# Interleaving two arrays: the store queue opens with loads in place of a tiny write

## The chip, the cores and the metric

The kernel runs on one core of one Trainium2 chip. The metric is device time in microseconds (us); where several executions were timed, the median is quoted with the lowest and highest.

## The reference

```python
def reference(x, y):                      # both (32, 256, 1024) float32
    result = np.zeros((batch, seq, dim * 2), dtype=np.float32)
    result[..., 0::2] = x
    result[..., 1::2] = y
    return result
```

The kernel reads 67.11 MB and writes 67.11 MB. There is no arithmetic.

## The kernel before

The arrays are flattened and cut into 8 tiles of 128 partitions by 8192 columns, 4.19 MB each. SyncE issues the loads of x and y, VectorE copies x into the even and y into the odd columns of an output tile (half an input tile at a time, so an output tile has 4.19 MB too), and ScalarE's sequencer (ACT) issues the stores. There are two buffers each for x, y and output.

```python
    xpool = ctx.enter_context(tc.tile_pool(name="xp", bufs=2))
    ypool = ctx.enter_context(tc.tile_pool(name="yp", bufs=2))
    opool = ctx.enter_context(tc.tile_pool(name="op", bufs=2))
    ...
    zero = wpool.tile([16, 128], fp32, name="zero")      # the early tiny write, 8 KB
    nc.vector.memset(zero, 0.0)
    first = dataclasses.replace(of, offset=0, ap=[[2 * WL, 16], [1, 128]])
    nc.scalar.dma_start(out=first, in_=zero)

    for lw in lwidths:
        ...
        nc.sync.dma_start(out=xtile, in_=xs)
        nc.sync.dma_start(out=ytile, in_=ys)
        while soff < lw:
            ...
            nc.vector.tensor_copy(out=otile[:, 0::2], in_=xsub)
            nc.vector.tensor_copy(out=otile[:, 1::2], in_=ysub)
            nc.scalar.dma_start(out=os_, in_=otile)
```

After compilation, the first load (x of the first tile) is moved ahead of the start barrier, into the opening block of SyncE.

## Time and profile before

| | before |
|---|---|
| time, median of 3 runs (lowest to highest) | 316.19 us (315.69 to 316.49) |
| span of the profiled execution | 313.8 us |
| the two queues' packets, share of 16 DMA engines | 99.4% |
| VectorE busy | 23% |
| first store issued, landed | 24.3 us, 48.1 us |

The table says that the 16 DMA engines are the bound and hardly ever idle. The page's lines and the stretches of the span that show it stand in the prediction below, with their reading. One more view belongs here, the timeline of the opening. Its columns are start, duration, engine, line, operation, output and input, count, and in brackets the wait before it.

```profile
12.28 4.50 DVE L70 COPY otile<-xtile 128x4096 f32<-128x4096 f32 x2 [11.25 <-DMA xtile<-in_x_dram]
...
22.00 4.50 DVE L71 COPY otile<-ytile 128x4096 f32<-128x4096 f32 x2 [5.22 <-DMA ytile<-in_y_dram]
24.32 33.66 ACTq L72 DMA_DIRECT2D out_dram<-otile  x3
```

VectorE copies x as soon as it is there, 10 us before y, and the first store is issued at 24.32, after the first copy of y.

### The profile page before, as it was taken

How to read it: one execution, taken by the hardware profiler on the slowest of the kernel's cores; microseconds unless marked ns; L12 is line 12 of the kernel's file. 1: busy time of each engine (PE TensorE's matmuls, PEld its weight loads, DVE VectorE, ACT ScalarE, POOL GpSimd, SP SyncE). 2: the span in 40 equal slices, each digit the busy share in tenths (PEclk: the TensorE clock that was granted, in tenths of full speed). 3: DMA queues.
4: the chain of work that ended last, by engine and by line, in shares of the span. 5: the costliest groups of instructions: out<-in, count | busy, mean ns of one | idle time of the engine just before them, and what ended most of it. 6: DMA issues, size and time to landing. Idle time of an engine off the chain costs nothing.

```text
span 313.8 us, 152 instructions
## 1 busy us (share of the span) xinstructions
DVE 72.8 (23%) x33; POOL 0.2 (0%) x4
## 2 busy tenths in 40 slices
DVE  0433002231032410325003150130501305023500
POOL 0000000000000000000000000000000000000000
DMA  8999999999999999999999999999999999999997
GB/s 339 464 405 397 468 401 464 405 464 405 464 405 464 405 459 409 451 418 451 418 434 434 430 439 426 443 413 455 401 468 401 468 401 468 401 468 401 464 405 334
DMA packets 4640, 134.23 MB, mean 428 GB/s; under 512 B 528, under 2 KB 544, under 8 KB 544
## 3 DMA queue, kind: packets, MB, share of 16 engines
q1 hardware_dynamic: 2304, 67.11, 49.9%
q10 hardware_dynamic: 2336, 67.12, 49.5%
HBM read 67.11 MB, written 67.12 MB: 428 GB/s over the span
## 4 chain that ended last, share of the span: by engine, by line
DMA 83%; DVE 11%; DVEq 1%; issue 0%
DMA out_dram<-otile 76%; DMA ytile<-in_y_dram 7%; DVE otile L71 6%; DVE otile L70 5%; DVEq L83 1%; DVEq L70 0%
## 5 line engine op out<-in xcount | busy, mean ns | idle before, releaser
L70 DVE COPY otile<-xtile 128x4096 f32<-128x4096 f32 x16 | 36.6, 2295 | 184.9 <-DMA out_dram<-otile 173.7
L71 DVE COPY otile<-ytile 128x4096 f32<-128x4096 f32 x16 | 36.6, 2292 | 39.8 <-DMA ytile<-in_y_dram 39.8
L45 DVE MEMSET zero<- 16x128 f32 x1 | 0.2, 165 | 0.9 <-PEq L119 0.9
L119 POOL MEMSET const-bfloat16-1.0<- 128x1 bf16 x1 | 0.1, 102 | 0.0
L119 POOL MEMSET const-uint8-127<- 128x1 uint8 x1 | 0.1, 102 | 0.0
L119 POOL MEMSET const-float32-0.0<- 128x1 f32 x1 | 0.1, 99 | 0.2 <-issue 0.2
L119 POOL MEMSET const-float32-1.0<- 128x1 f32 x1 | 0.1, 99 | 0.0
## 6 DMA issues: line engine op xcount, KB each, us to landing
out_dram<-otile ACTq DMA_DIRECT2D x16, 4096.0 KB, 29.1
xtile<-in_x_dram SPq DMA_DIRECT2D x8, 4096.0 KB, 43.6
ytile<-in_y_dram SPq DMA_DIRECT2D x8, 4096.0 KB, 60.7
out_dram<-zero ACTq DMA_DIRECT2D x1, 8.0 KB, 6.3
```

The costliest lines, as they stand in the source:

```text
L45: nc.vector.memset(zero, 0.0)
L70: nc.vector.tensor_copy(out=otile[:, 0::2], in_=xsub)
L71: nc.vector.tensor_copy(out=otile[:, 1::2], in_=ysub)
L83: tc.compile()
L119: nc = _bacc.Bacc("TRN2", target_bir_lowering=False, num_devices=1)
```

## The change

The intent: the ACT queue does useful work from the opening on, so the tiny write that opened it early is dropped. Both queues load from the start: x of the first tile on SyncE and y of the first tile on ACT, both ahead of the start barrier; then x and the second half of y of the second tile on SyncE, the first half of that y on ACT.

```diff
-    zero = wpool.tile([16, 128], fp32, name="zero")
-    nc.vector.memset(zero, 0.0)
-    first = dataclasses.replace(of, offset=0, ap=[[2 * WL, 16], [1, 128]])
-    nc.scalar.dma_start(out=first, in_=zero)
 ...
-        nc.sync.dma_start(out=xtile, in_=xs)
-        nc.sync.dma_start(out=ytile, in_=ys)
+        if t != 1:
+            nc.sync.dma_start(out=xtile, in_=rows(xf, start, lw))
+            yq = nc.scalar if t == 0 else nc.sync
+            yq.dma_start(out=ytile, in_=rows(yf, start, lw))
+        if t == 0:
+            nxt = start + P * lw
+            ...
+            nc.sync.dma_start(out=nx, in_=rows(xf, nxt, lw))
+            nc.scalar.dma_start(out=ny[:, :H], in_=rows(yf, nxt, lw, H))
+            nc.sync.dma_start(out=ny[:, H:], in_=rows(yf, nxt + H, lw, H))
 ...                                   # after compilation
-        if i.engine == mybir.EngineType.SP and i.opcode == "DMACopy"
+    for engine in (mybir.EngineType.SP, mybir.EngineType.Activation):
+        ...                           # the first DMA of each goes into its opening block
```

More of the change, by code (lines that the diff above doesn't have):

```diff
@@ L40, in _interleave, with rows @@
     assert sum(lwidths) == total // P
-    wpool = ctx.enter_context(tc.tile_pool(name="wp", bufs=1))
-    zero = wpool.tile([16, 128], fp32, name="zero")
-    nc.vector.memset(zero, 0.0)
-    first = dataclasses.replace(of, offset=0, ap=[[2 * WL, 16], [1, 128]])
-    nc.scalar.dma_start(out=first, in_=zero)
-    start = 0
-    for lw in lwidths:
-        xtile = xpool.tile([P, WL], fp32, name="xtile")[:, :lw]
-        ytile = ypool.tile([P, WL], fp32, name="ytile")[:, :lw]
-        xs = dataclasses.replace(xf, offset=start, ap=[[lw, P], [1, lw]])
-        ys = dataclasses.replace(yf, offset=start, ap=[[lw, P], [1, lw]])
-        nc.sync.dma_start(out=xtile, in_=xs)
-        nc.sync.dma_start(out=ytile, in_=ys)
-        soff = 0
-        while soff < lw:
-            width = min(WS, lw - soff)
-            otile = opool.tile([P, 2 * WS], fp32, name="otile")[:, : 2 * width]
+    H = WL // 2
+    def rows(flat, at, pitch, width=None):
+        return dataclasses.replace(flat, offset=at, ap=[[pitch, P], [1, width or pitch]])
+    start = 0
+    held = None
+    for t, lw in enumerate(lwidths):
+        if held is None:
+            xtile = xpool.tile([P, WL], fp32, name="xtile")
+            ytile = ypool.tile([P, WL], fp32, name="ytile")
+        else:
+            xtile, ytile = held
+            held = None
+        if t != 1:
[4 more added lines that the diff above has]
+            nxt = start + P * lw
+            nx = xpool.tile([P, WL], fp32, name="xtile")
+            ny = ypool.tile([P, WL], fp32, name="ytile")
+            nc.sync.dma_start(out=nx, in_=rows(xf, nxt, lw))
+            nc.scalar.dma_start(out=ny[:, :H], in_=rows(yf, nxt, lw, H))
+            nc.sync.dma_start(out=ny[:, H:], in_=rows(yf, nxt + H, lw, H))
+            held = nx, ny
+        for soff in range(0, lw, WS):
+            otile = opool.tile([P, 2 * WS], fp32, name="otile")
             os_ = dataclasses.replace(
@@ L65, in _interleave @@
                 offset=2 * start + 2 * soff,
-                ap=[[2 * lw, P], [1, 2 * width]],
+                ap=[[2 * lw, P], [1, 2 * WS]],
             )
-            xsub = xtile[:, soff : soff + width]
-            ysub = ytile[:, soff : soff + width]
-            nc.vector.tensor_copy(out=otile[:, 0::2], in_=xsub)
-            nc.vector.tensor_copy(out=otile[:, 1::2], in_=ysub)
+            nc.vector.tensor_copy(
+                out=otile[:, 0::2], in_=xtile[:, soff : soff + WS]
+            )
+            nc.vector.tensor_copy(
+                out=otile[:, 1::2], in_=ytile[:, soff : soff + WS]
+            )
             nc.scalar.dma_start(out=os_, in_=otile)
-            soff += width
         start += P * lw
@@ L86 @@
     blocks = nc.main_func.blocks
-    opening = blocks[0].instructions
-    at, moved = next(
-        (b, i)
-        for b in blocks[1:]
-        for i in b.instructions
-        if i.engine == mybir.EngineType.SP and i.opcode == "DMACopy"
-    )
-    assert not moved.sync_info.on_wait
-    body = at.instructions
-    body.remove(moved)
-    gate = next(
-        n
-        for n, i in enumerate(opening)
-        if i.engine == mybir.EngineType.SP and i.opcode == "Drain"
-    )
-    opening.insert(gate, moved)
-    at.instructions = body
-    blocks[0].instructions = opening
+    for engine in (mybir.EngineType.SP, mybir.EngineType.Activation):
+        opening = blocks[0].instructions
+        at, moved = next(
+            (b, i)
+            for b in blocks[1:]
+            for i in b.instructions
+            if i.engine == engine and i.opcode == "DMACopy"
+        )
+        assert not moved.sync_info.on_wait
+        body = at.instructions
+        body.remove(moved)
+        gate = next(
+            n
+            for n, i in enumerate(opening)
+            if i.engine == engine and i.opcode == "Drain"
+        )
+        opening.insert(gate, moved)
+        at.instructions = body
+        blocks[0].instructions = opening
 _INS = ['x', 'y']
```

## The prediction

> **What bounds the kernel now.** I read the page first: the row of DMA tenths, then the DMA queues, then the chain that ended last; after that the trace cut into stretches that begin and end on rows of transfers.
>
> The page, its slices and its queues:
>
> ```profile
> DVE  0433002231032410325003150130501305023500
> ...
> DMA  8999999999999999999999999999999999999997
> ...
> q1 hardware_dynamic: 2304, 67.11, 49.9%
> q10 hardware_dynamic: 2336, 67.12, 49.5%
> HBM read 67.11 MB, written 67.12 MB: 428 GB/s over the span
> ```
>
> The reader is to see that the DMA engines are 90% busy or more in every slice but the first and the last, while VectorE, the only computing engine, is at 23%. The two queues' packets took 49.9 + 49.5 = 99.4% of 16 engines' 313.8 us, that is 311.9 us. The kernel moves each byte once in and once out, and the change moves the same ones (but for 8 KB).
>
> The chain that ended last, on the page:
>
> ```profile
> DMA 83%; DVE 11%; DVEq 1%; issue 0%
> DMA out_dram<-otile 76%; DMA ytile<-in_y_dram 7%; DVE otile L71 6%; DVE otile L70 5%; DVEq L83 1%; DVEq L70 0%
> ```
>
> The chain names VectorE for 11%, but this is a trap: it follows one buffer from hand to hand, and while VectorE copies, the DMA engines carry other transfers (the slices show it). What ends the kernel is the time the 16 engines need for 134.23 MB, plus the moments in which they move nothing or are slow.
>
> Those moments come from the stretches. Columns: the stretch, its length, VectorE, GpSimd, clock, DMA share (1.00 is all 16 engines busy), GB/s.
>
> ```profile
> 0.00:0.90 0.90, 0.04 (x1) 0.20 (x4) 1.00 0.00 0
> 0.90:4.05 3.15, 0.13 (x1) 0.00 (x0) 1.00 0.99 333
> 4.05:25.80 21.75, 8.30 (x4) 0.00 (x0) 1.00 1.01 434
> 25.80:29.05 3.25, 0.69 (x1) 0.00 (x0) 1.00 0.94 323
> 29.05:312.60 283.55, 63.61 (x28) 0.00 (x0) 1.00 1.00 433
> 312.60:313.80 1.20, 0.00 (x0) 0.00 (x0) 1.00 0.00 0
> ```
>
> Loads alone run at 434 GB/s, loads beside stores and stores alone at 433: one ceiling whatever the mix. At 433 GB/s the data takes 134.23 / 0.433 = 310.0 us. The rest is four losses: 0.9 us before the first packet; 3.15 x (1 - 333/433) = 0.73 us in the first row of packets; 3.25 x (1 - 323/433) = 0.83 us where the first large store enters; 1.2 us after the last packet. Sum 313.7, the span to 0.1. So everything that any re-ordering can win is 3.7 us, or 1.2%, and this change touches about half of that.
>
> **What the Trainium skill says.** "DMA: Bandwidth & Descriptors", section "Where 436 GB/s comes from", puts the ceiling of the 16 ports at 435.2 GB/s; the trace agrees with 433 to 434. The same page, "Issuing engines are not separate DMA queues", says that transfers issued from several engines run on the same 16 DMA engines and interleave, and that issuing from several only saves the sequencer's time. The trace agrees: one queue alone (4.05 to 25.80) and two together (29.05 on) have the same rate. The same page, "Queues, rings and completion order", says that an engine takes turns between its queues, a packet at a time; the before fits that (the first store, issued at 24.32, landed by 48.1, some 24 us, where alone it would have had 4.19 MB / 0.433 = 9.7). I use it below to place transfers.
>
> **The change, part by part.** The order of instructions on each engine shows what moves. Removed: a VectorE memset (0.17 us, beside the DMA) and the tiny 8 KB write. Moved: y0 from SyncE to the opening of the ACT queue; the first half of y1 onto the ACT queue, the second half last on SyncE. VectorE's first four copies go from x, x, y, y to x, y, x, y. From the second tile on all stays.
>
> (1) *Bytes.* 8 KB less of 134.23 MB: 0.02 us at 433 GB/s. y1 in halves makes 128 more packets (8 per engine) of 16 KB instead of 32. With 4640 packets in all and the four losses explaining all but 0.1 us, a packet's fixed cost must be small: if all of that 0.1 were fixed cost, 290 packets per engine would have 0.3 ns each. I set +0.05 us as a generous estimate. Net 0.
>
> (2) *First data.* Before, x0 alone lands at 12.3 and y0 at 22.0. After, x0 and y0 take turns and both land near 22 (same 8.39 MB, 19.4 us, after the same start). VectorE starts its first copy about 10 us later, and the first store can be issued after two copies of 2.29 us, less their overlap 4.5 us: at 26.5 instead of 24.3. No DMA time is lost by it, because both queues still hold loads: x1 and both halves of y1, 8.39 MB or 19.4 us, until about 41.
>
> (3) *First store.* It stands behind the first half of y1 in the ACT queue. From 22, x1 (4.19 MB) and that half (2.10 MB) take turns: 6.29/0.433 = 14.5 us, both done near 36.5. Then the second half and store 0: 14.5 us, to 51. Then x2 and store 1, y2 and store 2, and so on, 19.4 us each. So the first store enters at 36 instead of 29, and the kernel is behind in stores by 7 us or so, and ahead in loads by as many bytes.
>
> (4) *The tail.* Following the pairs, x2 with store 1 ends at 51 + 19.4 = 70.4, and eleven more pairs bring y7 in at 70.4 + 11 x 19.4 = 284 (before: 287.7). Three stores remain, 3 x 9.7 = 29.1, to 313. The store of the first half of tile 7 is issued 4.5 us after 284, while store 13 runs until 293.5; the last is issued 4.5 us after 293.5, while store 14 runs until 303. Slack 5 us at each: the queue doesn't run dry, the tail costs nothing.
>
> (5) *The entry of the store queue*, the only place where I expect a gain. The 0.83 us at 25.80 to 29.05 comes once, when the ACT queue gets its first large transfer; later stores have no such dip. After, that queue is at work from the opening on. If the loss belongs to the queue's waking, it goes or coincides with SyncE's own 0.73 at the start: -0.8. If it belongs to the first write to HBM, it stays. I can't tell from the before, and take half: -0.4.
>
> (6) *The start.* ACT issues y0 in about 0.4 us beside SyncE's x0, which has 0.37; the start barrier may go back by 0.1, which only later issues feel. The 0.9 us before the first packet and the 1.2 us at the end stay.
>
> Sum: 0.0 + 0.0 + 0.0 + 0.0 - 0.4 + 0.0 = -0.4 us on 316.19: **315.8 us**.
>
> **The rivals.** *A: the whole dip goes.* For it: it occurs once and at the queue's first large transfer. Against: the tiny write had already woken the queue at about 5 us and the dip came all the same. Time: 315.4. *B: the tiny write did pay.* It may have spared the first store a longer stall, which now comes back at 36 us: for it, that someone put it in; against, that a y load has the queue moving by then. The dip would double, +0.8: 317.0. *C: two loads in turn are slower than one load stream*, through HBM or through both queues opening cold: the stretch of loads alone lasts from 1 to 36 us; 1% less rate there is +0.35, a second cold row +0.7: 316.5 to 316.9. For it, nothing but that no such stretch is in the before; against, that every mix there runs at 433. *D: VectorE, waiting until 22 us for its first input, becomes a bound.* It is busy for 72.8 us of 313.8 and its copies need 9.2 us of each 38.7 us tile; the shift of 10 us would have to reach the store queue while that is empty, and by (3) it isn't. Nothing.
>
> **Range and chances.** A gives the low side (315.4, and by the spread of the runs before, 315.69 to 316.49, about 0.4 lower: 315.0), B and C the high side (316.9). Faster by over 2% means under 309.9 us, below the 310.0 that the data alone needs: 1%, left for an effect on the DMA rate itself. Slower by over 2% is over 322.5: it needs 6 us of idle DMA, which the placing of transfers excludes unless I have a dependence wrong: 2%. Within 2%: 97%.
>
> **What would show it.** In the stretches of the changed kernel: no packet before 0.9; a first row at about 330 GB/s; 433 to 434 from there to the first store; at about 36 us a dip to 320 GB/s over 3 us (it stayed) or none (A); 433 to the last 1.2 us. The waits: VectorE waits some 21 us once for x or y at the start. The first store issued near 26.5, landing near 51; the last store issued 14 us before the end. The queues' share summed should be 99.4 to 99.8%. Wrong would be a stretch of over 1 us with the DMA idle in the middle or the tail, a rate between 1 and 36 us other than 433, or two slow first rows.

## The result

| | before | after |
|---|---|---|
| time, median of 6 runs (lowest to highest) | 316.03 us (315.69 to 316.49) | 316.12 us (316.01 to 316.28) |
| span of the profiled execution | 313.8 us | 314.4 us |
| first store issued, landed | 24.3, 48.1 us | 26.4, 52.4 us |
| y of the last tile is there | 287.7 us | by 284.9 us |

The ratio is 1.0002, with a 95% interval of 0.9989 to 1.0015: the same time. (A ratio here is the mean time of one kernel's fast runs over that of the other's in the same rounds, so it isn't quite the ratio of the medians quoted.) The after is no faster, but it is steadier: its six runs lie within 0.27 us, those of before within 0.80 us. The profile of before had fallen on one of its fastest executions (315.62 us), which makes the spans look further apart than the medians are.

The last row of the table rests on these two lines, the first copy that needs y of the last tile before, and the first copy of the last tile after. The latter waited for an output buffer, so its input was there earlier:

```profile
287.67 2.29 DVE L71 COPY otile<-ytile 128x4096 f32<-128x4096 f32 x1 [4.92 <-DMA ytile<-in_y_dram]
284.86 2.29 DVE L79 COPY otile<-xtile 128x4096 f32<-128x4096 f32 x1 [14.95 <-DMA out_dram<-otile]
```

The page of the changed kernel, slices, packets and queues:

```profile
DVE  0029003205041050410505004050140502305500
...
DMA  9999999999999999999999999999999999999997
...
DMA packets 4752, 134.22 MB, mean 427 GB/s; under 512 B 528, under 2 KB 528, under 8 KB 528
...
q10 hardware_dynamic: 2592, 73.40, 54.2%
q1 hardware_dynamic: 2160, 60.82, 45.2%
```

The DMA row is 9 everywhere but in the last slice, VectorE starts in the third slice instead of the second, and the ACT queue (q10) now carries 54.2% against 45.2% on SyncE's (q1). The sum, 99.4%, is that of before.

The same cut into stretches as the prediction has for the kernel before (stretch, length, VectorE, GpSimd, clock, DMA share, GB/s):

```profile
0.00:0.90 0.90, 0.00 (x0) 0.20 (x4) 1.00 0.00 0
0.90:3.93 3.03, 0.00 (x0) 0.00 (x0) 1.00 0.99 346
3.93:33.60 29.67, 8.90 (x4) 0.00 (x0) 1.00 1.00 433
33.60:37.10 3.50, 0.00 (x0) 0.00 (x0) 1.00 1.05 300
37.10:313.25 276.15, 62.96 (x28) 0.00 (x0) 1.00 1.00 432
313.25:314.40 1.15, 0.00 (x0) 0.00 (x0) 1.00 0.00 0
```

Loads alone on two queues run at 433 GB/s for 30 us. The dip at the first store has moved from 26 to 34 us and is still there: 3.50 x (1 - 300/433) = 1.08 us, against 0.83 before. The slow first row of packets has shrunk a little: 3.03 x (1 - 346/433) = 0.61 us, against 0.73.

And the opening of the changed kernel in its timeline:

```profile
0.12 0.38 ACTq L62 DMA_DIRECT2D ytile<-in_y_dram  x1
...
21.84 2.30 DVE L79 COPY otile<-xtile 128x4096 f32<-128x4096 f32 x1 [21.84 <-DMA xtile<-in_x_dram]
...
26.37 50.32 ACTq L85 DMA_DIRECT2D out_dram<-otile  x4
```

VectorE waits 21.84 us once, since x and y of the first tile now arrive together, and the first store is issued 2 us later than before.

**A finer reading of the same traces.** A stretch cuts through rows of packets, because the 16 engines do not run in step. The trace has every packet with its start and duration, and an engine's next packet starts where its last one ended (up to 4 ns before), so the packets can be strung into 16 chains. A packet of 32 KB takes 1.213 us in all traces when nothing disturbs it (one of 16 KB takes 0.611), and in the kernel before each engine has exactly 256 of them: 310.5 us. What an engine takes above that is its own loss. For the dip I sum that loss from 20 to 45 us. The end of each chain is marked by that engine's completion of the last store. Which chain a packet belongs to is not certain where two engines end within a few ns of each other, so a loss is not given engine by engine; the mean and the ends do not depend on it. In its place stands the time of the slowest packet in the dip above its usual 1.213 or 0.611. In us (the mean dip is some 0.06 low, since packets overlap by a few ns):

```
kernel            first store   dip per engine   slowest packet,   end of the 16 engines    span
                  enters        mean             above usual       median   last
before (fast run)   29.1        0.58             0.67              312.41   312.70          313.8
after               37.1        1.14             0.78              312.92   313.24          314.4
```

In the kernel before 21 packets are stretched in the dip, in the changed kernel 46, by about as much each. In both they are loads, and all of them start before the first packet of the first store does: between 25.9 and 27.7 us for a first store packet at 29.10, and between 33.6 and 36.7 us for one at 37.11. The 2048 store packets of the kernel before took 1.213 us each. So the dip "at the first store" is time that the loads just ahead of it lose; why they lose it is not shown. The kernel ends with its last engine, in both profiles about 0.3 us after the median one.

### The profile page after: what moved, and what is told of

Read it like the earlier page. It is cut to its first block, busy times and chain, and to the rows that moved or that the text cites. A ratio compares the mean times of both kernels' runs of the same rounds, so it can differ in the third digit from the quotient of the medians.

```text
span 314.4 us, 150 instructions
## 1 busy us (share of the span) xinstructions
DVE 71.9 (23%) x32; POOL 0.2 (0%) x4
## 3 DMA queue, kind: packets, MB, share of 16 engines
q10 hardware_dynamic: 2592, 73.40, 54.2%
q1 hardware_dynamic: 2160, 60.82, 45.2%
## 4 chain that ended last, share of the span: by engine, by line
DMA 74%; DVE 11%; issue 10%; DVEq 1%
DMA out_dram<-otile 67%; DMA xtile<-in_x_dram 7%; DVE otile L79 6%; DVE otile L82 5%; DVEq L95 1%; DVEq L79 0%
## 5 line engine op out<-in xcount | busy, mean ns | idle before, releaser
L79 DVE COPY otile<-xtile 128x4096 f32<-128x4096 f32 x16 | 36.7, 2295 | 226.9 <-DMA out_dram<-otile 160.5
```

The lines of the kernel that those rows point to most:

```text
L79: nc.vector.tensor_copy(out=otile[:, 0::2], in_=xtile[:, soff : soff + WS])
```

## The experiments

The open questions after the result: what the dip is, why it grew, and why the kernel before spreads more from run to run. Each experiment is described by its difference from one of the two kernels. "Dip" and "end" are worked out from the packets as above. Runs with 5 rounds have a median over 4 to 6 fast runs; the others are single, and I use their profiles, not their times.

**No tiny write, nothing else** (from before).

```diff
-    zero = wpool.tile([16, 128], fp32, name="zero")
-    nc.vector.memset(zero, 0.0)
-    nc.scalar.dma_start(out=first, in_=zero)
```

> The kernel before without its tiny write, nothing else. In the kernel before the dip where the first large store enters costs 0.8 us (3.25 us at 323 GB/s against 433); in the changed kernel 1.1 us (3.5 us at 300 GB/s). Theory 1, the dip belongs to the first write to HBM and the tiny write had paid a part of it: the dip grows to 1.1 us or more, time 0.3 to 0.5 us up. Rival 2, the dip belongs to the waking of the ACT queue: without the tiny write the first store wakes it alone, 1.5 us or more (the slow first row of loads, 0.73, on top). Rival 3, the changed kernel's larger dip is due to its 16 KB packets: here the dip stays at 0.8 us and the time within 0.1 us of before.

Measured: 315.92 us (315.59 to 316.88), ratio to before 0.9999 (0.9984 to 1.0014). Mean dip 0.69 us, last engine at 312.64. The tiny write had been doing nothing that can be seen: without it the dip neither doubled (theories 1 and 2) nor did the time move. Rival 3, the 16 KB packets, was left by this run alone.

**The tiny write put back** (from after), right behind the first y tile on ACT.

> The changed kernel with the tiny write put back, right behind the first y tile on the ACT queue. Theory 1, the tiny write pays part of the dip in advance: the dip at the first store falls from 1.1 to 0.8 us, time 0.3 us under the changed kernel. Rival 2 (waking of the queue) and rival 3 (16 KB packets): the dip stays at 1.1 us and the time at that of the changed kernel.

Measured: 316.24 us (316.11 to 316.29), ratio to before 1.0004 (0.9992 to 1.0016). Mean dip 1.13 us, as in the changed kernel. Theory 1 falls from this side too. (In this position the tiny write stands behind 4 MB of loads and enters near 22 us, still well before the first store at 38.3.)

**y of the second tile whole on SyncE** (from after): no 16 KB packets.

```diff
-            nc.scalar.dma_start(out=ny[:, :H], in_=rows(yf, nxt, lw, H))
-            nc.sync.dma_start(out=ny[:, H:], in_=rows(yf, nxt + H, lw, H))
+            nc.sync.dma_start(out=ny, in_=rows(yf, nxt, lw))
```

> The changed kernel with y of the second tile whole, last on the SyncE queue: only the first y tile opens the ACT queue, no 16 KB packets, no tiny write. The first store should enter right at the end of the first pair of tiles, near 31 us in place of 37. Theory 1 (first write): dip of 1.1 us, as in the changed kernel. Rival 3 (16 KB packets): 0.8 us. Time between 315.8 and 316.3 in either case.

Measured: 316.14 us (315.95 to 316.35), ratio 1.0004 (0.9991 to 1.0017). The first store was expected to enter near 31 us; three engines had it by 30.7, the others from 31.8 on. Mean dip 1.17 us: the 16 KB packets aren't the reason either, and the second half of the change, splitting that y, moves nothing in the time.

**Stores that stop and enter again in mid-run**, first attempt (from before): a one-column copy from x of the sixth tile ahead of the fifth tile's copies.

> The kernel before in which the copies of the fifth tile wait until x of the sixth has landed, so that the ACT queue runs empty in mid-run while loads go on alone from about 184 to 195 us, and stores then enter again. Theory 1, the dip belongs to the first write of the execution: no dip at the second entry, rate 433 GB/s throughout. Rival 2, it belongs to the waking of an empty queue, or rival 4, to the change from loads alone to loads and stores: a second dip of 0.7 us or more near 195 us, and the time up by that. The dip near 27 us stays at 0.8 us in all.

This run tested nothing: the scheduler placed all copies of the fifth tile ahead of that small copy, so the stores never stopped. It is, in effect, the kernel before with one 0.15 us copy more. One look gave 317.09 us and a profile that turned out useful: mean dip 1.02 us, but two packets in it took 2.93 and 3.11 us (1.72 and 1.89 above the usual), and the last engine ended at 313.89 where the median engine ended at 312.64.

**The kernel before once more**, for a second profile.

> The kernel before, unchanged, for a second profile. The kernel before spreads over 315.6 to 316.7 us from run to run where the changed one stays within 316.0 to 316.4, and its first profile fell on a fast run (315.6). If the spread comes from the dip at the first store, a slower run shows a larger dip than 0.8 us there and the same 433 GB/s elsewhere; if it comes from elsewhere, the dip is 0.8 us again and another stretch is slower.

Measured: 316.57 us in one look. The stretches of this profile:

```profile
4.05:25.80 21.75, 8.15 (x4) 0.00 (x0) 1.00 1.00 433
25.80:29.10 3.30, 0.84 (x1) 0.00 (x0) 1.00 1.00 318
29.10:312.60 283.50, 63.62 (x28) 0.00 (x0) 1.00 1.00 433
```

The rates are those of the fast execution. By packets, the mean dip is 0.83 us, but one packet in it took 3.04 us (1.83 above the usual), and the last engine ended at 313.64 while the median ended at 312.56. So this execution of before was 0.95 us longer than the fast one (315.62), and 0.94 us of that is the last engine's end (313.64 against 312.70), although the median engine was only 0.15 us later. A rate over all engines hides this: one engine of 16 that is 1 us behind takes 0.02% from the mean.

**Stores that stop and enter again, forced** (from before).

```diff
+            if t == 4 and soff == 0:      # held = the loads of tile 5, issued early
+                nc.vector.tensor_copy(out=otile[:, :2], in_=held[0][:, :2])
             nc.vector.tensor_copy(out=otile[:, 0::2], in_=xsub)
```

> The re-entry again, now forced: the first copy of the fifth tile's output waits for x of the sixth tile (in the run before it the copies had been placed ahead of the wait, so nothing was tested). The ACT queue should be empty from about 184 us for 8 us or more while loads go on alone. If the dip belongs to the first write of the execution: none at the second entry. If it belongs to an empty queue's waking or to the change from loads alone to loads beside stores: a second dip of 0.6 us or more, and the time up by that.

Measured, in one look: stores stopped at 182 and entered again at 197 us; from 182 to 197 us every packet in the trace is a load. The stretch across the second entry:

```profile
183.50:213.50 30.00, 9.03 (x5) 0.00 (x0) 1.00 1.01 436
```

There is no dip at the second entry; every packet from 182 to 214 us took 1.213 us. So at this entry neither the waking of an empty store queue nor the change from loads alone to loads beside stores cost anything. But the same run has an entry that did cost. The delay later left the load queue empty from 234 us on, and loads entered again at 243 us:

```profile
238.00:252.00 14.00, 3.85 (x3) 0.00 (x0) 1.00 1.01 403
```

Here 34 packets, 29 of them loads, were stretched between 241 and 251 us, by 1.1 us per engine on average (14 x (1 - 403/433) = 0.97 by the stretch). The last engine ended at 315.43 and the median at 313.61, and the run took 318.63 us. So an entry in mid-run is not always free, and what tells the two apart stays open.

**A large early write from HBM to HBM in place of the tiny one** (from before).

```diff
-    nc.scalar.dma_start(out=first, in_=zero)                      # [16, 128]
+    nc.scalar.dma_start(out=first, in_=the same 16 rows of x)     # [16, 8192]
```

> The kernel before with a large early write in place of the tiny one: one row of 32 KB for each DMA engine, copied from x straight to the output, issued at 1 us (later overwritten). It adds 1.2 us of transfer. If the dip is a cost of the first large write to HBM, it moves to about 5 us and the first store at 29 us enters without one: time 1.2 us up, 317.2. If it belongs to the entry of a stream of stores, the dip at 29 us stays as it was: again 1.2 us up or a little more, with two places of loss.

Measured: 317.68 us (317.31 to 317.91), ratio 1.005 (1.0038 to 1.0063). Around the early write and around the first store:

```profile
4.00:7.60 3.60, 0.00 (x0) 0.00 (x0) 1.00 1.01 437
27.00:30.30 3.30, 0.84 (x1) 0.00 (x0) 1.00 0.98 318
```

The early write entered at 5.2 us on an idle queue at full rate, and the dip at 29 us stayed (mean 0.78). The first large write to HBM isn't what costs. By the ratio the time rose by 1.6 us: 1.2 for the added packet, and in the profiled run the last engine ended 0.67 us after the median (314.38 and 313.71), for 0.29 in the fast run of before.

**An eighth of the first y tile on ACT** (from before, no tiny write).

```diff
+            nc.scalar.dma_start(out=ytile[:, :E], in_=ya)         # E = WL // 8
+            nc.sync.dma_start(out=ytile[:, E:], in_=yb)
```

> The kernel before without the tiny write, with an eighth of the columns of the first y tile as a load on the ACT queue; from 5 us on that queue is empty until the first store, as before. If the larger dip of the changed kernel comes from the ACT queue having carried loads, the dip is 1.1 us or more here too and the times are narrow around 316.1. If it comes from two queues of loads being deep in flight shortly before the store, the dip is as in the kernel before, 0.6 to 0.8 us at best, and the times spread from 315.6 up.

Measured: 315.79 us (315.70 to 316.43), ratio 0.9998 (0.9984 to 1.0011). Mean dip 0.70 us. Having carried loads doesn't make the ACT queue pay more at its first store.

**A later first store on one load queue** (from before): the first copies wait for y too.

```diff
+            if start == 0:
+                nc.vector.tensor_copy(out=otile[:, :2], in_=ysub[:, :2])
             nc.vector.tensor_copy(out=otile[:, 0::2], in_=xsub)
```

> The kernel before whose first copies wait for the first y tile too, as they do in the changed kernel: copies in the order x, y, x, y from 22 us on, first store issued near 26.5, all loads on one queue, tiny write kept. The dip of the three kernels of the changed kind was 1.1 us on average over the 16 engines, that of the kernel before and its variants 0.6 to 0.8. If the later and differently ordered first store makes the dip larger: 1.1 us here too, times narrow around 316.1 or somewhat above. If the two queues of loads make it larger: 0.6 to 0.8 here, times from 315.6 up, spread over 1 us.

Measured: 319.46 us (319.22 to 319.65), ratio 1.0105 (1.0092 to 1.0119). Neither side had expected this. Mean dip 0.95 us, near that of the changed kernel. The 3 us come from somewhere else, the last microseconds. First this run, then the kernel before, in the stretch after 312 us:

```profile
312.00:313.00 1.00, 0.00 (x0) 0.00 (x0) 1.00 0.16 66
313.00:316.00 3.00, 0.00 (x0) 0.00 (x0) 1.00 0.05 22
```

```profile
312.00:313.00 1.00, 0.00 (x0) 0.00 (x0) 1.00 0.01 0
```

In the kernel before no packet of data starts after 312 us. Here 66 GB/s over 1 us are two packets of 32 KB and 22 GB/s over 3 us are two more (0.066 MB each): two engines still at work. The median engine ended at 312.77, the last but one at 313.91 and the last at 315.89. Two packets of the dip took 2.40 and 2.58 us, and after it there are 21 slow packets of 1.26 to 1.59 us on the store queue between 40 and 90 us, 3.6 us above the usual 1.213 together.

**The first columns stored early** (from before, no tiny write): 1024 columns of the first tile loaded, copied and stored by themselves.

```diff
+            for lo, hi in ((0, E), (E, lw)):
+                for flat, tl in ((xf, xtile), (yf, ytile)):
+                    nc.sync.dma_start(out=tl[:, lo:hi], in_=part)
 ...
-            width = min(WS, lw - soff)
+            width = E if start + soff == 0 else WS - soff % WS
```

> The kernel before without the tiny write; the first 1024 columns of the first tile are loaded, copied and stored by themselves, so that a real store of 8 KB rows from SBUF enters near 10 us; the other 3072 columns of that half follow. Same bytes. An early write from HBM to HBM left the dip at 29 us in place, and so did the tiny one. If the dip is the cost of the first store from SBUF of more than a few hundred bytes, it moves to near 10 us and the later stores enter at full rate; if it hangs on rows of 32 KB entering, it stays near 29 us. Should the small store's dip be smaller, the time is 0.3 to 0.5 us under before, at best 315.5; if there are two dips, 316.5.

Measured: 317.30 us (317.00 to 321.40), ratio 1.0059 (1.0024 to 1.0095). The stretch up to the early store's entry at 9.7 us, then loads alone, then the entry of the large stores at 31 us:

```profile
0.90:9.70 8.80, 1.39 (x2) 0.00 (x0) 1.00 1.03 357
19.90:31.10 11.20, 6.26 (x3) 0.00 (x0) 1.00 1.02 440
31.10:60.00 28.90, 4.54 (x2) 0.00 (x0) 1.00 1.01 435
```

The dip at 31 us is gone: the large stores enter after 11 us of loads alone at full rate. Up to 9.7 us, 8.80 x (1 - 357/433) = 1.54 us are lost, 0.8 more than the slow first row alone costs in before. This fits a dip that belongs to the first store from SBUF of some size and has moved with it. It isn't a clean test: packets that began before the early store was issued at 5.48 us are stretched too, up to 2.72 us, and the first loads of this run are smaller, so how much of the 0.8 us is the store's isn't shown. As a way to save time it failed: the median engine ended at 312.84 and the last at 313.95, both later than in the fast run of before.

**The late store without the tiny write**, to stand against the changed kernel in one thing.

> The late first store of the run before on one load queue, now without the tiny write, so that it stands against the changed kernel with y of the second tile whole (316.14 us) in one thing: the first y tile is on the SyncE queue instead of the ACT queue. The late store with the tiny write took 319.5 us, because one DMA engine of 16 ended 3 us after the others. If the single load queue makes that straggler, about 319 us again; if the tiny write had a part in it, 316.0 to 316.5.

Measured: 316.84 us (316.26 to 319.54), ratio 1.004 (1.0013 to 1.0067). The six runs are 316.26, 316.33, 316.39, 317.29, 317.34 and 319.54. Mean dip in the profiled run (316.39) 0.97 us. One load queue with a late store can end as early as the changed kernel, but doesn't do so reliably; with the tiny write all four runs were worse (319.2 at best), which I can't explain. The kernel with y whole, which has the first y tile on ACT instead, stayed within 315.95 to 316.35.

**Halves of the first tile on both queues** (from after), an attempt to beat both.

```diff
+                for lo in (0, H):
+                    nc.sync.dma_start(out=xtile[:, lo : lo + H], in_=rows(xf, lo, lw, H))
+                    nc.scalar.dma_start(out=ytile[:, lo : lo + H], in_=rows(yf, lo, lw, H))
```

> An attempt at a version better than both: the first tile in column halves, x on SyncE and y on ACT, the second tile whole on SyncE. The first store can be issued near 16 us instead of 26 and two queues load from the opening on. If a late first store is what makes the dip 1.1 us, and two queues are what keeps the 16 engines together, the dip is 0.7 us, no engine straggles, and the time is 0.4 us under the changed kernel, 315.6 to 315.8 with a narrow spread. If the dip belongs to the two queues, 316.1 as the changed kernel.

Measured: 317.67 us (317.38 to 317.90), ratio 1.0048 (1.0035 to 1.0061). The first store was issued at 16.1 us and entered at 24.2; the dip came out as hoped, 0.68 us. But two new losses took its place:

```profile
62.00:67.00 5.00, 4.98 (x3) 0.00 (x0) 1.00 1.01 400
290.00:300.00 10.00, 6.29 (x3) 0.00 (x0) 1.00 0.92 393
```

Near 65 us stores had been away for 6 us and there is a second dip, 0.4 us (this entry, too, was not free); and at the end the store queue ran dry. The line of the timeline that shows why:

```profile
291.09 2.30 DVE L85 COPY otile<-ytile 128x4096 f32<-128x4096 f32 x1 [7.35 <-DMA ytile<-in_y_dram]
```

y of the last tile came at 291.1 us, where the kernel before has it at 287.7 and the changed one by 284.9. Stores that start earlier run ahead, loads arrive later by as many bytes, and at the end too few stores were queued to bridge the last copies: 10 x (1 - 393/433) = 0.9 us. The last engine ended at 314.92, the median at 313.81.

**The runs side by side**, by packets (us):

```
kernel           first load    first store   mean   slowest   end of engines     times
                 queue(s)      enters        dip    packet    median    last     lowest to highest
before (fast)    one           29.1          0.58   0.67      312.41   312.70    315.5  to 316.7
before again     one           29.2          0.83   1.83      312.56   313.64    (one look)
b_reentry        one           29.3          1.02   1.89      312.64   313.89    (one look)
b_no_tiny        one           29.1          0.69   0.73      312.48   312.64    315.59 to 316.88
b_act_eighth     1/8 of y0     29.1          0.70   0.77      312.52   312.77    315.70 to 316.43
b_late_no_tiny   one           31.7          0.97   0.91      312.73   313.04    316.26 to 319.54
b_late_store     one           31.6          0.95   1.37      312.77   315.89    319.22 to 319.65
after            two           37.1          1.14   0.78      312.92   313.24    316.01 to 316.28
a_tiny           two           38.3          1.13   0.91      312.85   313.13    316.11 to 316.29
a_y1_whole       two           30.4          1.17   0.82      312.80   313.02    315.95 to 316.35
a_halves         two, halves   24.2          0.68   0.71      313.81   314.92    317.38 to 317.90
```

The three runs with an added entry (b_reentry2, b_big_early, b_small_first) are left out. The lowest and highest of before are over the 11 and 12 runs that stood beside these experiments. Their medians were 315.91 to 316.23 us.

## Why the prediction was right

The time lay 0.3 us above the predicted 315.8 and inside the range; "within 2%" was right. That rests on the reading of the bound. The expected gain of 0.4 us did not come (it lies just outside the interval of the ratio, which reaches down to 0.9989, or 0.35 us), and that the number came out close all the same is partly luck: the one step with a gain in it failed, and the steps are small against the range. By its own steps:

**The bound** was read rightly. Both kernels keep the 16 engines at 432 to 433 GB/s from the first store to the end, and no order of the same transfers can win more than about 1%.

**Steps 2, 3 and 4** came out to within a microsecond or so. The first store was expected to be issued at 26.5 and to land near 51, and had 26.4 and 52.4; it entered at 37.1 for an expected 36.5. y of the last tile was expected at 284 and was there by 284.9. The last store was issued at 298.8, for some 298 in step 4 (its list of signs has "14 us before the end", which does not fit its own times; it was 15.6), and no stretch in the middle or the tail was idle. The halves experiment shows that the tail was worth checking: there the same reasoning, not made, cost 0.9 us.

**Step 1** holds: with the 16 KB packets taken away (y whole on SyncE) the time is 316.14 us (in other rounds) against 316.12. Its 0.3 ns for a packet's fixed cost was a misreading, though, since such a cost is hidden in the rate of 433 GB/s: two packets of 16 KB take 2 x 0.611 us for 1.213, so 8 pairs cost an engine 0.07 us for the 0.05 allowed.

**Step 6** holds for the 0.9 us before the first packet and the end of 1.15. The slow first row, which it left as it was, shrank by 0.12 us by the stretches (0.73 to 0.61).

**Step 5, the entry of the store queue, failed.** It expected a gain of 0.4 us, half of a dip that would go if it belonged to the waking of the ACT queue. The dip didn't shrink but grew, from 0.58 us on average in the fast run of before (0.83 in the slower one) to 1.14, though the queue had been at work since the opening. The 0.83 that the prediction halved was itself a stretch's reading; by packets that execution lost 0.58. That the ACT queue's waking makes the dip is refuted from several sides: an early write and an early load on the idle queue entered without loss, and stores that entered again at 197 us paid nothing. What the runs show in its place is a loss of the loads just ahead of the first store from SBUF of some size; with an early store of 1 MB, the dip at 31 us was gone (one run, and not a clean one). It isn't a price paid only once: b_reentry2 lost 1.1 us near 247 us and a_halves 0.4 near 65. It is 0.58 to 1.02 us on average where the first store entered by 30.3 us (b_big_early is the latest of these) and 0.95 to 1.17 where it entered later. The two ranges overlap, and the late entries differ in other things too (load queues, order of the copies), so that a late entry makes it larger is not shown, and why it grew stays open.

**Rival B**, that the tiny write had spared the first store a stall, predicted a larger dip and got one, but for the wrong reason: taking the tiny write from before and giving it to after left each kernel's dip and time where they were. Rival A fell with step 5. Rival C fell too: from 3.93 to 33.60 us the loads of two queues ran at 433 GB/s, and there was one slow first row, not two. So did D: the queues did not run empty.

**What the prediction had left out** is that the kernel ends with the slowest of 16 engines. It reckoned with a mean rate. The changed kernel's median engine ends 0.5 us later than in the fast run of before (312.92 against 312.41), about what the larger dip, less the better first row, gives. Yet the medians of the times differ by only 0.1 us. A likely reason is that in some executions of before one engine or a few fall behind in the dip, by single packets of some 3 us: the last engine ended 1.08 us after the median in the second profile of before and 1.25 us after it in its near-copy b_reentry, against 0.32 in the changed kernel (and 0.29 in the fast run of before). That the other slow runs of before are of this kind is inferred from these two; no other run of before has a profile. As far as these profiles go, the change exchanges a small loss with an occasional straggler for a larger loss that all engines share. That the two queues of loads are what keeps the engines together is supported by one comparison with a late store, first y on SyncE (316.26 to 319.54, with two copies of 0.1 us more) against first y on ACT (315.95 to 316.35), without a profile of the slow ones; a_halves, with two queues as well, had its last engine 1.1 us behind, so it is no guarantee. Why a single engine falls behind, and why the tiny write made the late store worse, stays open.

No experiment beat both kernels clearly. The best, an eighth of the first y tile on ACT and no tiny write, had 315.79 us and a ratio to before of 0.9998, which is the same.

## What to carry to other kernels

When the DMA engines are full from first packet to last, re-ordering transfers can only win what the stretches at the start, at the first store and at the end lose; add those up before trying, and here the sum was 3.7 us of 314. Compare the last engine with the median one, since a mean rate doesn't show a straggler, and use more than one profile of a kernel whose times spread. Starting the stores earlier isn't free: it makes the loads later, and the tail needs enough stores in the queue to bridge the last copies.

## What the Trainium skill lacked or had wrong

- "DMA: Bandwidth & Descriptors", section "Where 436 GB/s comes from", is confirmed as a ceiling (435.2 GB/s stated, 432 to 434 measured over long stretches, with loads alone and with loads beside stores).
- The same page, section "Issuing engines are not separate DMA queues", says that issuing from several engines only saves sequencer time. The mean rate agrees, but with a late first store the times differ: 316.26 to 319.54 us (six runs) with the first y tile on one queue with x, and 315.95 to 316.35 (five runs) with it on the other. That this comes from how the 16 engines stay together isn't shown, since the slow ones have no profile.
- No page that I read has the loss of the loads just ahead of the first store from SBUF: 0.6 to 1.2 us per engine, whatever the queue had done before, and absent for an early write from HBM to HBM and at a second entry of stores at 197 us. Two later dips, 0.4 us near 65 us in a_halves and 1.1 us near 247 us in b_reentry2, are unexplained.
- The same page, section "Why a DMA increments its semaphore by 16 and not by 1", says that the engines of a transfer finish independently, but gives no size. Here the last engine of 16 ended 0.2 to 3.1 us after the median engine, and between two profiles of the kernel before that difference makes 0.8 of the 0.95 us by which their times differ.
